# A sixth pair of rows by seven quarter products in the first MLP product, and later sums of its activations

## The chip, the cores and the metric

One core of a Trainium2 chip runs one layer of a streaming encoder in float32, in one launch. The metric is the device time of that launch in microseconds.

## The reference

The layer has token mixers, a cross-attention and a gated MLP. The change lies in the MLP, on 512 tokens of 1024 channels, with 2816 gate and 2816 value channels:

```python
hf = _rms_norm(x, norm_ffn_pre[l])
u = _dwconv_causal(hf @ w_up[l], ffn_dw[l]) + ffn_dw_b[l]      # width 3
u_g, u_v = jnp.split(u, 2, axis=-1)
yff = (jax.nn.silu(u_g) * u_v) @ w_down[l]
x = x + _rms_norm(yff, norm_ffn_post[l])
```

## The kernel before

Every operand of a matrix product is split in a high part (a cast, `wh`, `hth`) and a remainder (`wl`, `htl`), and a product is three matmuls: high x high, high x remainder, remainder x high. ScalarE (ACT) makes the cast (L191 for weights), VectorE (DVE) the remainder (L192).

**The first product, `up_jobs`.** It runs over 22 rows `j`. A row has two blocks of 128 channels, gate and value; a plain block (`plain_jobs`) is 8 slices of the 1024 inputs by three matmuls over 512 tokens, in one PSUM bank taken from `mm` and `av` in turn. `done` then applies the width-3 convolution (an activation on ACT, two taps on DVE, L597), and at the value block `gated` multiplies silu(gate) by value into `ns.quart[j // 2]` (tiles `qa0` to `qa10`, one for two rows).

**Pairs, `seven_jobs`.** At a row in `SEVEN_AT` the blocks of gate and value are seen as a 2 x 2 matrix (gate and value by two halves of the inputs) times a 2 x 2 matrix (halves of inputs by halves of tokens). Seven quarter products, each 4 slices by three matmuls over 256 tokens, take the place of eight: `A11`, `A12`, `S2`, `S3`, `S1`, `S4`, `A22`. The weights' sums `su`, `wv`, `s` (L1692 to L1695) are formed on DVE from the raw weights `wg` and `wv`; the tokens' sums are formed once, in `token_terms`, and split in `split_terms` into tiles `t4` to `t7`, `res0` to `res2` and `qa10`. Products are added up in three banks (`sc` twice, `tr`) and taken out to `u` by copies on ACT and adds on DVE (L1685). The jobs of such a row are mixed with the two plain blocks of the row after it, so a pair covers rows `j` and `j + 1`. The first pair's raw weights are loaded by `load_pair` two rows ahead, those of the next in `second_weights`.

**Sums of `w_down`, class `Sums`.** The last product is also done by seven products in place of eight. Its weight sums are formed during the first product, in 33 steps (`load`, `add` on DVE L545 to L548, `store` to DRAM L552, on POOL's queue), each placed by a call of `step()` after a job's products. Raw weights, `su`, and the rows of `w_down` (`wp`, later `dw`) share one ring of seven tiles (`ring`).

**Activation sums, `quart_sums`.** For two rows `q` the last product needs x1 + x3, x0 - x1 and (x1 + x3) - x0 of the four quarters of `ns.quart[q]` (L1598 to L1600, DVE, 256 wide). They go to `term_tile`s. Before the change they start two rows after the last pair.

**The last product, `down_jobs`.** Phase 0 forms M1, M6, M5 and M7 over 11 steps `q` with two jobs each; phase 1 forms M2, M3 and M4, and `ends` adds them up, multiplies by the gain `ns.post`, adds the residual `ns.out` (loaded again by `reload`) and stores. `weights` and `activations` make the splits (L1808, L1809), `load` issues the loads on SP (L564) three jobs ahead.

**Order.** `run_blocks` calls each job's weights three jobs ahead of its products. The text of the program gives the priority; a planner, which computes due times of its own, decides the order of the instructions on each engine and each queue. `tc.issue_after` keeps an instruction behind a named one. An engine takes its instructions in the planned order, and so does SP with its loads.

Of the kernel before, what the change touches and what calls it, by code (L numbers as in the profile page):

```python
# [25 lines left out]
P = 128  # L26
# [10 lines left out]
WB = 2 * 520  # L37
LINE = 256
HALF_SHIFT = 16
SEVEN_AT = (5, 8, 11, 14, 17)  # L40
BIG = -float(2.0 ** 100)
LAMBDA_INIT = 0.8 - 0.6 * math.exp(-0.3 * 0)

# [41 lines left out]
def hybrid_layer(ctx: ExitStack, tc: tile.TileContext, a: dict, out: bass.AP):  # L85
    nc = tc.nc
    V, A, G, PE, SP = nc.vector, nc.scalar, nc.gpsimd, nc.tensor, nc.sync
# [10 lines left out]
    def bank(tag=None):  # L98
        if tag is None:
            turn_of.n += 1  # L100
            tag = "av" if turn_of.shared and turn_of.n % 2 else "mm"
        return psum.tile([P, 512], F32, tag=tag, name=f"ps_{tag}", bufs=2)
# [143 lines left out]
    def channel_major(ps, w, act, sl=slice(0, S)):  # L246

        hi, lo = w
        nk = hi.shape[1]
        for k in range(nk):  # L250
            mm3(ps[:, sl], hi[:, k, :], lo[:, k, :], act[0][:, k, sl], act[1][:, k, sl], k == 0, k == nk - 1)
            if k == 3 < nk - 1:
                bg.tick()
# [324 lines left out]
    def seven_banks(phase):  # L578
        names = (("M2", "sc"), ("M3", "tr"), ("M4", "mm")) if phase else (("M1", "sc"), ("M6", "tr"), ("M5", "mm"),
                                                                         ("M7", "av"))  # L580
        return {name: [bank(tag) for _ in range(2)] for name, tag in names}
# [543 lines left out]
    ns = SimpleNamespace()  # L1125
# [425 lines left out]
    def open_ffn():  # L1551
        bg.drain("n1")
        token_terms()
        close(ns.work_)
        close(ns.xp_)
        close(ns.xm_)
        ns.fp_, ns.fp = new_pool("ffn", False)
        ns.work = ns.fp
        ns.quart = [quart(q) for q in range(NF // 2 - 1)]

    def term_tile(i, dtype=F32):
        if i < NT:
            return ns.res.tile([P, 4, S // 2], dtype, tag=f"res{i}", name=f"t{i}")
        return ns.fp.tile([P, 4, S // 2], dtype, tag=f"t{i}", name=f"t{i}")
# [13 lines left out]
    def split_terms():  # L1578
        for i, places in enumerate(((4, 5), (6, 7), (0, 1), (2, None))):
            hi, lo = (quart(10, F32R) if n is None else term_tile(n, F32R) for n in places)  # L1580
            split(ns.terms[i], hi, lo)
            ns.terms[i] = hi, lo

    def quart_sums(n, behind):

        if ns.quart_sums is None:
            ns.quart_terms = [term_tile(i) for i in range(6)]
            ns.post = ns.quart_terms.pop().rearrange("p a b -> p (a b)")
            ns.quart_sums = []
            G.dma_start(ns.post, a["norm_ffn_post"][0].partition_broadcast(P))  # L1590
        for q in range(len(ns.quart_sums), min(n, NF // 2)):
            x = ns.quart[q]
            if q < 10:
                two = ns.quart_terms[q // 2][:, q % 2 * 2:q % 2 * 2 + 2]
            else:
                two = ns.fp.tile([P, S], F32, tag="s4", name="two").rearrange("p (a b) -> p a b", a=2)
            with tc.issue_after(behind):
                V.tensor_tensor(two[:, 0], x[:, 1], x[:, 3], ALU.add)  # L1598
                V.tensor_tensor(two[:, 1], x[:, 0], x[:, 1], ALU.subtract)
            V.tensor_tensor(x[:, 1], two[:, 0], x[:, 0], ALU.subtract)  # L1600
            ns.quart_sums.append(two.rearrange("p a b -> p (a b)"))
# [4 lines left out]
    def up_jobs():  # L1606
        st, held = {}, []
        seven = SEVEN_AT
        raws = {}
# [13 lines left out]
        def done(j, i, ps):  # L1623
            if i == 0:
                st[j] = ns.fp.tile([P, 2, S], F32, tag="c", name="c", bufs=2)
            first_and_taps(st[j], j, i, ps)
            if i == 1:
                gated(st[j], j)
# [14 lines left out]
        def step(n=1):  # L1643
            for _ in range(n):
                f, q = next(steps, (None, None))
                if f == ns.sums.add:
                    with tc.issue_after(st["taps"]):
                        f(q)
                elif f is not None:
                    f(q)  # L1650
# [6 lines left out]
        def plain(j, i):  # L1657
            return cols(w_up, i * DFF + j * P)

        def load_pair(j):  # L1660
            if j in seven:
                raws[j] = [ring(name="wg"), ring(name="wv")]
                for i, raw in enumerate(raws[j]):
                    SP.dma_start(raw.rearrange("p (k c) -> p k c", k=NK), plain(j, i)[0])

        def seven_jobs(j):
# [10 lines left out]
            def product(ps, name, b, first=True):  # L1677
                hi, lo = w[name]
                for k in range(4):
                    for i, (w_p, x_p) in enumerate(((hi, b[0]), (hi, b[1]), (lo, b[0]))):  # L1680
                        matmul(ps[:, :S // 2], w_p[:, k], x_p[:, k], first and i == k == 0, i == 2 and k == 3,
                               not first)

            def add(dst, ps):
                V.tensor_tensor(dst, dst, ps[:, :S // 2], ALU.add)  # L1685
# [25 lines left out]
            def first(_):  # L1711
                u = kept["u"] = ns.fp.tile([P, 2, 2, S // 2], F32, tag="u", name="u", bufs=2)
                x.update(x=bank("sc"), v=bank("sc"), w=bank("tr"))
                product(x["x"], "A11", old(0, 0))
                A.copy(u[:, 0, 0], x["x"][:, :S // 2])
                step()
                product(x["w"], "A12", old(1, 0))
                add(u[:, 0, 0], x["w"])

# [41 lines left out]
        def plain_jobs(j):  # L1761
            for i in range(2):
                def body(hi, lo, i=i):
                    if j > 1:
                        ps = bank()
                        channel_major(ps, (hi, lo), ns.hf)
                        done(j, i, ps)
                        if (j, i) == (seven[0] - 2, 0):
                            load_pair(seven[0])
                        if (j, i) >= (seven[0] - 2, 1):  # L1770
                            step()
                        if j > seven[-1] + 1:
                            quart_sums(2 * (j - seven[-1] - 2) + i + 1, st["taps"])
                        return
                    if (j, i) == (0, 0):
                        bg.drain("n0")
                    ps = bank(("mm", "sc")[i])
                    (channel_major if i or j else by_pass)(ps, (hi, lo), ns.hf, slice(0, S // 2))
                    held.append((j, i, ps, (hi, lo)))
                    if (j, i) == (1, 1):  # L1780
                        open_ffn()
                        for m, n, ps, w in held:
                            (channel_major if m or n else by_pass)(ps, w, ns.hf, slice(S // 2, S))
                            done(m, n, ps)
                        split_terms()
                yield *plain(j, i), body, V, same, HALF_SHIFT if j < 2 else 0

        j = 0
# [6 lines left out]
    def down_jobs():  # L1795
# [11 lines left out]
        def split_to(hi, lo, x):  # L1807
            A.copy(hi, x)  # L1808
            parts["low"] = V.tensor_tensor(lo, x, hi.bitcast(F32), ALU.subtract).ins  # L1809

        def reload():
            ns.out = [term_tile(t).rearrange("p a b -> p (a b)") for t in range(NT)]
            for t in range(NT):
                SP.dma_start(ns.out[t], ns.kept[t * P:(t + 1) * P, :])
# [150 lines left out]
        def body(phase, q, job, ws):  # L1965
            if (q, job) == (0, 0):
                banks.update(seven_banks(phase))
            if (phase, q, job) == (1, 2, 0):
                reload()
            if phase == 0 and job == 0:  # L1970
                quart_sums(len(ns.quart_sums) + 1, parts["low"])
            if phase and q >= pairs - hold:
                held.append((q, job, ws))
                if (q, job) == (pairs - 1, 1):
                    ends()
                return
            for (name, a), w in zip(SEVEN[phase, job], ws):
                for t in range(2):
                    step(name, t, q, a, w, phase)
            if (phase, q) == (0, pairs - 1):  # L1980
                middle(job)
# [51 lines left out]
```

## Time and profile before

| what | value |
| --- | --- |
| median of 3 runs | 1048.98 us (1048.38 to 1055.58) |
| the profiled execution | 1049.11 us, of which span 1047.3 us |
| TensorE (PE) | 1038.0 us busy, 99% |
| weight load (PEld) | 891.0 us, 85% |
| VectorE (DVE) | 832.9 us, 80% |
| ScalarE (ACT) | 527.1 us, 50% |
| GpSimd (POOL) | 167.2 us, 16% |
| moved by DMA | 167.31 MB, mean 160 GB/s |

An engine that is busy for 99% of the span sets the time; the others matter where they make it wait. Shares over the span hide the stages, so the MLP, from about 700 us to the end, is read by stretches.

### The profile page before, as it was taken

What the parts mean: (1) busy time and instruction counts of PE and PEld (TensorE: products, weight loads), DVE (VectorE), ACT (ScalarE), POOL (GpSimd) and SP (SyncE); (2) the same over time, 40 slices, a digit from 0 to 9 for tenths busy, and PEclk for the clock granted to TensorE, in tenths of its full rate; (3) what the DMA queues carried; (4) which work ended last, traced back from release to release, by engine and by line L of the source; (5) the groups of instructions that cost most, each with busy time, mean ns of one, the idle gap of its engine ahead of it and who ended that gap; (6) DMA issues with size and microseconds to landing.
All of it is one profiled execution on the core that took longest, in us unless ns stands there. A gap on an engine that the chain in (4) does not pass through costs nothing.

```text
span 1047.3 us, 15070 instructions
## 1 busy us (share of the span) xinstructions
PE 1038.0 (99%) x5475; PEld 891.0 (85%) x5475; DVE 832.9 (80%) x1377; ACT 527.1 (50%) x888; POOL 167.2 (16%) x309
## 2 busy tenths in 40 slices
PE   9999999999999999999999999999999999999997
PEld 8888888888888988888888899999888888888886
DVE  6899997667667567767577798788787898799896
ACT  5322222277465365655444565666444454455672
POOL 4000000300231334343011031030011120000001
PEclk9999999999999999999999999999999999999999
DMA  8854334652443363332358733246478777827652
GB/s 269 289 172 104 103 101 139 181 123 81 120 122 95 88 173 93 99 97 65 121 161 231 269 124 122 100 143 196 123 245 246 255 240 235 269 83 266 189 176 81
DMA packets 166529, 167.31 MB, mean 160 GB/s; under 512 B 6656, under 2 KB 136301, under 8 KB 166198
## 3 DMA queue, kind: packets, MB, share of 16 engines
q1 hardware_dynamic: 154147, 124.10, 39.4%
q0 software_dynamic: 12160, 42.10, 12.3%
q8 instruction: 43, 0.70, 0.3%
q14 instruction: 33, 0.26, 0.1%
q10 hardware_dynamic: 146, 0.14, 0.0%
HBM read 141.13 MB, written 25.18 MB: 159 GB/s over the span
## 4 chain that ended last, share of the span: by engine, by line
PE 89%; DMA 4%; DVE 3%; issue 3%; ACT 0%; POOL 0%; SPq 0%; POOLq 0%; DVEq 0%; ACTq 0%
PE ps_mm L233 46%; PE ps_av L233 25%; PE ps_sc L233 10%; PE ps_tr L233 4%; PE ps_tr L237 2%; DMA sums<-wp 2%; DMA wr<-in_w_up 1%; DVE wl L192 1%; DVE c L597 1%; PE ps_mm L445 1%; PE ps_av L445 1%; PE ps_mm L387 0%; PE ps_sc L392 0%; ACT wh L191 0%; POOL wp L541 0%
## 5 line engine op out<-in xcount | busy, mean ns | idle before, releaser
L191 ACT CAST wh<-wr 128x1024 fp32r<-128x1024 f32 (+1 forms) x132 | 138.3, 1050 | 241.3 <-PE ps_mm L233 130.3
L192 DVE TENSOR_TENSOR wl<-wr,wh 128x1024 fp32r<-128x1024 f32 (+1 forms) x132 | 163.6, 1240 | 60.6 <-ACT wh L191 60.2
L233 PE MATMUL ps_mm<-hth,wh 128*128 128x512 f32 (+1 forms) x552 | 205.7, 380 | 0.2 <-ACT hth L156 0.2
L233 PE MATMUL ps_mm<-htl,wh 128*128 128x512 f32 (+1 forms) x552 | 205.3, 379 | 0.0
L233 PE MATMUL ps_mm<-hth,wl 128*128 128x512 f32 (+1 forms) x552 | 205.1, 379 | 0.0
L233 PEld LDWEIGHTS ps_mm<-hth,wl 128*128 128x128 f32 x552 | 102.0, 188 | 18.8
L233 PEld LDWEIGHTS ps_mm<-hth,wh 128*128 128x128 f32 x552 | 102.1, 188 | 18.2 <-ACT hth L156 0.8
L233 PEld LDWEIGHTS ps_mm<-htl,wh 128*128 128x128 f32 x552 | 102.1, 188 | 17.5
L233 PE MATMUL ps_av<-hth,wh 128*128 128x512 f32 (+1 forms) x312 | 116.3, 373 | 0.0
L233 PE MATMUL ps_av<-htl,wh 128*128 128x512 f32 (+1 forms) x312 | 116.2, 373 | 0.0
L233 PE MATMUL ps_av<-hth,wl 128*128 128x512 f32 (+1 forms) x312 | 116.1, 372 | 0.0
L668 DVE SCALAR_TENSOR_TENSOR y<-y,par,y 128x482 f32<-128x482 f32 (+29 forms) x120 | 83.2, 734 | 0.1
L233 PEld LDWEIGHTS ps_av<-hth,wl 128*128 128x128 f32 x312 | 58.6, 188 | 10.2
L233 PEld LDWEIGHTS ps_av<-htl,wh 128*128 128x128 f32 x312 | 58.6, 188 | 10.2
L233 PEld LDWEIGHTS ps_av<-hth,wh 128*128 128x128 f32 x312 | 58.6, 188 | 10.1
L1809 DVE TENSOR_TENSOR wl<-dw,wh 128x1024 fp32r<-128x1024 f32 x32 | 39.0, 1220 | 3.0 <-ACT wh L1808 2.2
L1061 POOL TENSOR_SCALAR fbias<-ck,cq 128x128 f32<-128x128 f32 (+3 forms) x32 | 28.2, 889 | 62.8 <-DVE st L1068 56.4
L1808 ACT CAST wh<-dw 128x1024 fp32r<-128x1024 f32 x32 | 33.4, 1049 | 9.2 <-PE ps_tr L233 6.6
L156 ACT CAST pth<-ps_tr 128x512 fp32r<-128x512 f32 (+3 forms) x56 | 23.5, 448 | 24.6 <-PE ps_tr L237 24.5
L269 POOL TENSOR_TENSOR st_m<-pm,nhalf 128x1 f32<-128x1 f32 x12 | 3.4, 287 | 180.3 <-ACT junk L1874 111.3
L157 DVE TENSOR_TENSOR ptl<-ps_tr,pth 128x512 fp32r<-128x512 f32 (+3 forms) x56 | 27.5, 512 | 5.7 <-ACT pth L156 5.3
L1619 ACT ACTIVATE c<-c 128x512 f32<-128x512 f32 x22 | 13.9, 631 | 35.7 <-DVE c L597 35.7
(553 smaller groups left out, 2418.5 us busy)
## 6 DMA issues: line engine op xcount, KB each, us to landing
wr<-in_w_in SPq DMA_DIRECT2D x38, 512.0 KB
wr<-in_w_up SPq DMA_DIRECT2D x34, 512.0 KB
wr<-in_w_gate SPq DMA_DIRECT2D x32, 512.0 KB
wp<-in_w_down POOLq DMA_DIRECT2D x22, 512.0 KB, 6.3
sums<-wp POOLq DMA_DIRECT2D x22, 512.0 KB, 5.0
dw<-sums SPq DMA_DIRECT2D x44, 256.0 KB
wr<-in_w_branch SPq DMA_DIRECT2D x16, 512.0 KB
wide<-in_w_out SPq DMA_DIRECT2D x12, 512.0 KB
```

What stands on the lines that cost most here:

```text
L156: A.copy(hi, ps)
L157: V.tensor_tensor(lo, ps, hi.bitcast(F32), ALU.subtract)
L191: order(A.copy(hi, raw[:, :n]))
L192: low.tensor_tensor(lo, raw[:, :n], hi.bitcast(F32), ALU.subtract)
L233: PE.matmul(ps, lhs, rhs, start=start, stop=stop, skip_group_check=more)
L237: PE.transpose(ps, x, ident[:n, :n])
L445: keep(PE.matmul(banks[c][:, :S // 2], w[p == 1][:, k, c * P:(c + 1) * P], ht[p == 2][:, i * 4 + k, :S // 2], start=(i, p, k) == (0, 0, 0) ...
L668: ins = V.scalar_tensor_tensor(dst[:, s:], src[:, :S - s], pc("conv_dw", k * 4 + j), dst[:, s:], ALU.mult, ALU.add)
L1061: G.tensor_scalar(bias[:, :w], ck[j][:, :w], -1.0, cq[:, qt, head:head + 1], ALU.mult, ALU.add)
L1619: A.activation(c[:, 0], c[:, 0], AF.Silu)
L1808: A.copy(hi, x)
L1809: parts["low"] = V.tensor_tensor(lo, x, hi.bitcast(F32), ALU.subtract).ins
```

## The change

A sixth pair is done by seven quarter products, and the pairs begin one row earlier. In `first` of a pair one `step()` goes. `quart_sums` takes tiles one by one (3, 6, 7, 0, 1), is called for two row pairs in the row ahead of the last pair and for two more in the row behind it, and leaves the rest to the last product. The load of the gain `norm_ffn_post` goes from the first call of `quart_sums` to step 5 of phase 0, into tile 5.

```diff
-SEVEN_AT = (5, 8, 11, 14, 17)
+SEVEN_AT = (4, 7, 10, 13, 16, 19)
...
         if ns.quart_sums is None:
-            ns.quart_terms = [term_tile(i) for i in range(6)]
-            ns.post = ns.quart_terms.pop().rearrange("p a b -> p (a b)")
-            ns.quart_sums = []
-            G.dma_start(ns.post, a["norm_ffn_post"][0].partition_broadcast(P))
+            ns.quart_terms, ns.quart_sums = [], []
         for q in range(len(ns.quart_sums), min(n, NF // 2)):
             x = ns.quart[q]
             if q < 10:
+                if q % 2 == 0:
+                    ns.quart_terms.append(term_tile((3, 6, 7, 0, 1)[q // 2]))
                 two = ns.quart_terms[q // 2][:, q % 2 * 2:q % 2 * 2 + 2]
...
                 product(x["x"], "A11", old(0, 0))
                 A.copy(u[:, 0, 0], x["x"][:, :S // 2])
-                step()
                 product(x["w"], "A12", old(1, 0))
...
                             step()
-                        if j > seven[-1] + 1:
-                            quart_sums(2 * (j - seven[-1] - 2) + i + 1, st["taps"])
+                        if j == seven[-1] - 1:
+                            quart_sums(i + 1, st["taps"])
+                        if j > seven[-1]:
+                            quart_sums(i + 3, st["taps"])
...
+        def load_post():
+            ns.post = term_tile(5).rearrange("p a b -> p (a b)")
+            G.dma_start(ns.post, a["norm_ffn_post"][0].partition_broadcast(P))
...
                 banks.update(seven_banks(phase))
+            if (phase, q, job) == (0, 5, 0):
+                load_post()
             if (phase, q, job) == (1, 2, 0):
                 reload()
```

## Prediction

> **What bounds the kernel now.** I read the page first, then a table of stretches cut at the stages of the MLP, then the order of time on the tensor engine, and last the waits of PE, SP and DVE around the pairs that the change touches.
>
> ```profile
> span 1047.3 us, 15070 instructions
> PE 1038.0 (99%) x5475; PEld 891.0 (85%) x5475; DVE 832.9 (80%) x1377; ACT 527.1 (50%) x888; POOL 167.2 (16%) x309
> L191 ACT CAST wh<-wr 128x1024 fp32r<-128x1024 f32 (+1 forms) x132 | 138.3, 1050 | 241.3 <-PE ps_mm L233 130.3
> ```
>
> TensorE is busy for 1038.0 of 1047.3 us. The question is thus only how much matrix work goes away and whether PE starts to wait anywhere for what replaces it. By stretches (one pair of the first product with the plain row behind it, the fifth pair, the plain rows 19 to 21, phase 0 of the last product):
>
> ```profile
> core 0: us, PE busy (x) PEld busy (x) DVE busy (x) ACT busy (x) POOL busy (x), PEclk, DMA share, GB/s
> 753.70:785.40 31.70, 31.70 (x181) 27.90 (x180) 26.55 (x37) 14.60 (x20) 4.27 (x8) 1.00 0.66 217
> ...
> 848.80:880.50 31.70, 31.70 (x182) 27.83 (x181) 27.35 (x39) 15.00 (x21) 4.81 (x9) 1.00 0.85 278
> 880.50:902.20 21.70, 21.40 (x131) 18.74 (x130) 16.94 (x24) 8.03 (x13) 2.67 (x5) 1.00 0.78 252
> 902.20:934.90 32.70, 32.70 (x150) 27.18 (x149) 28.61 (x45) 15.81 (x22) 0.00 (x0) 1.00 0.45 135
> 934.90:994.90 60.00, 60.00 (x266) 49.53 (x265) 53.39 (x80) 39.87 (x57) 0.00 (x0) 1.00 0.67 214
> ```
>
> PE is busy through each of them but for 0.3 us in the fifth pair. DVE is the next engine: 26.55 us of 31.70 in the first pair's stretch, 27.35 in the fourth, 28.61 of 32.70 in the three rows at the end, 53.39 of 60.00 in phase 0 of the last product. ACT stays at half in the first product and two thirds in phase 0. The DMA share climbs to 0.85 while the sums of w_down are loaded and stored beside the weights, and is 0.45 in the last three rows. The one wait of PE that the view of waits shows in this whole part, and the chain that leads to it:
>
> ```profile
> PE ps_sc L233 <- DVE u L1685: 0.3, 1, 0.3
> ```
>
> ```profile
> 886.12 3.56 DMA sums<-wp
> 889.68 0.02 SPq L564
> ...
> 891.00 6.95 DMA wr<-in_w_up
> ...
> 898.03 1.06 ACT wh L191
> ...
> 899.12 1.23 DVE wl L192
> ...
> 901.00 0.34 DVE u L1685
> ...
> 901.38 1.65 PE ps_sc L233 x12
> ```
>
> The reader is to see here a store of sums (886.12) that a load on SP (L564) waits for, because the load takes the ring slot which the store empties; behind that, in the same queue, a weight load of the first product (891.00, 6.95 us), then its cast on ACT, its remainder on DVE (899.12), DVE's add into u behind that (901.00), and PE 0.3 us late. So before the change the lead of the weights in the fifth pair is already used up, and the price was 0.3 us.
>
> **The change part by part.**
>
> *One more pair, minus two plain rows.* Rows 4/5, 7/8, 10/11, 13/14, 16/17 and 19/20 become pairs, where 5/6, 8/9, 11/12, 14/15 and 17/18 were. A plain row is two blocks of 24 matmuls over 512 tokens; the first row of a pair is 7 products of 12 matmuls over 256 tokens.
>
> ```profile
> 748.39 5.44 PE ps_av L233 x24
> 753.83 1.41 PE ps_sc L233 x12
> ```
>
> By these rows a block is 5.44 us, so a row is 10.88; a quarter product is 1.41, so seven are 9.87, and the pair saves 10.88 - 9.87 = 1.01 us. A second way takes the pairs themselves, by the first matmul of product A11 in the first, the second and the fifth:
>
> ```profile
> 753.66 0.28 PE L233 MATMUL ps_sc<-hth,wh 128*128 128x256 f32 x1
> ...
> 785.42 0.28 PE L233 MATMUL ps_sc<-hth,wh 128*128 128x256 f32 x1
> ...
> 880.50 0.28 PE L233 MATMUL ps_sc<-hth,wh 128*128 128x256 f32 x1
> ```
>
> From the first to the fifth are 126.84 us for four periods, 31.71 each; less a plain row of 10.88, a pair takes 20.83 us in place of 21.76. That is 0.93 us saved, and it holds whatever small waits a pair brings with it. I take -0.93; the bounds are -0.88 (the first period alone, 31.76) and -1.01.
>
> A rule of the Trainium skill speaks against cutting matmuls shorter: "TensorE: Matmul & The Clock Gate", section "Wait — 56ns, not 53.3ns?", says that a warm matmul takes its columns at 2.4 GHz plus about 2.5 ns, however many columns there are. By its figures, as an estimate, 48 x 215.8 ns less 84 x 109.2 ns would leave a gain of 1.19 us. The trace has such a fixed cost and a larger one (1.41 / 12 = 117.5 ns and 5.44 / 24 = 226.7 ns, so 8.3 ns for each matmul cut in two), so the rows decide.
>
> *What the added pair asks of DVE and ACT.* Beside a plain row, the first row of a pair has one more remainder over 1024 (three in place of two), one over 512 (s4l), four sums of weights over 512 and three adds of 256 into u; its four taps and its product remain.
>
> ```profile
> L192 DVE TENSOR_TENSOR wl<-su,wh 128x1024 fp32r<-128x1024 f32 x5 | 6.1, 1220 | 0.9 <-ACT wh L191 0.9
> L1685 DVE TENSOR_TENSOR u<-u,ps_sc 128x256 f32<-128x256 f32 x10 | 4.1, 414 | 0.0
> L1693 DVE TENSOR_TENSOR su<-su,wg 128x512 f32<-128x512 f32 x5 | 3.5, 690 | 0.1
> L157 DVE TENSOR_TENSOR s4l<-s,s4h 128x512 fp32r<-128x512 f32 x5 | 3.4, 683 | 0.0
> L1599 DVE TENSOR_TENSOR t<-qa 128x256 f32<-128x256 f32 x5 | 2.1, 420 | 0.0
> L1598 DVE TENSOR_TENSOR t<-qa 128x256 f32<-128x256 f32 x5 | 2.1, 415 | 0.0
> L1600 DVE TENSOR_TENSOR qa<-t,qa 128x256 f32<-128x256 f32 x4 | 1.7, 421 | 0.0
> ```
>
> That is 1.22 + 0.68 + 4 x 0.69 + 3 x 0.41 = 5.9 us of DVE, an upper value, since each instruction's record reaches a little into the next. Of the activation sums (L1598 to L1600, 0.42 + 0.42 + 0.42 = 1.26 us for a row pair) six were placed in the rows after the last pair and four are now, so 2.5 us go from this product to the last. The cover in rows 19 to 21 is 32.70 - 28.61 = 4.1 us of idle DVE; the need is 5.9 - 2.5 = 3.4 us. It fits by 0.7 us, which is thin. In phase 0 of the last product 53.39 + 2.5 = 55.9 us of 60.0 stand. It fits too, because the sums no longer have to come early: each phase 0 step of the last product asks for one, and the four ahead are four steps of lead. Cost taken: 0. If the cover in the rows is gone, the late thing would be the taps of row 21, which still read the PSUM bank that M7 or M5 needs, and the price is the whole shortage of up to 5.9 - 4.1 = 1.8 us. ACT gets one more cast of 1.05 us, a half one and four short copies, with 17 us idle in 32.7: 0.
>
> *The sums of w_down.* A step less in `first` makes four steps for a pair in place of five; the first step comes a row earlier (row 2). Counting the 33 steps through the rows, the last store was issued in the fifth pair's second job (row 17/18) and will be issued in row 18, ahead of the sixth pair. Between pairs there are six steps per three rows in place of seven, so the crowded stretches (DMA share 0.85) lose a seventh of the sums' traffic and of DVE's work on them. What moves the other way is the end: the last two stores now fall just ahead of the last pair, whose two raw weights and their sum also sit in the same seven-slot ring (`dw`), and the first loads of the last product must wait for these slots.
>
> ```profile
> SPq L564 <- DMA sums<-wp: 8.1, 4, 3.7
> ```
>
> Four such waits are there now, 8.1 us in all on SP, with nothing on PE beyond the stall shown. The weights queued behind L564 on SP are those of the plain rows; two tiles (`wr`) of lead cover them. Bounds: -0.3 us (the present stall disappears because the traffic is thinner) to +3.7 us (one longest wait, uncovered, next to the last pair). I take 0, nearest to the rows, since waits of 8.1 us have cost only that stall.
>
> *Where sums and gain lie.* The sums go to tiles 3, 6, 7, 0 and 1 in place of 0 to 4. Tile 3 is empty after the splits; 6, 7, 0 and 1 hold terms of products S2 and S3, done before row 21. The row pair 10 takes the tile of A22's low term while A22 is still to come in the sixth pair, so the product of row 20 waits for A22; that is one quarter product (1.41 us) right behind row 20's last matmuls, shorter than row 20's own taps on DVE, behind which its product stands anyway. If it did wait, u's add, the taps of row 19 and the remainder of row 21's weights would queue behind it on DVE, for at most 1.41 us. I take 0. The reload of the residual waits longer for tiles 0 and 1, but it is used only in the tail. 0.
>
> *The output gain* goes from the end of the sums to step 5 of phase 0.
>
> ```profile
> t<-in_norm_ffn_post POOLq DMA_DIRECT2D x1, 512.0 KB, 9.2
> ```
>
> Its 9.2 us are needed after step 10, five steps of 5.4 us later. 0. POOL has nothing queued behind it there: its next work in the page is in the second phase.
>
> *The sum.* The profiled execution took 1049.11 us with a span of 1047.3, so 1.8 us lie around it; its own time is 0.13 above the median of 1048.98. 1049.11 - 0.93 = 1048.2 us for the changed kernel, against the median a difference of -0.8.
>
> **The rivals.**
>
> 1. *The stall goes too.* Sums thinner by a seventh leave the weight loads of the pairs on time; the pair's -0.93 and the 0.3 us of the chain both go: 1047.9; with what a pair takes beyond its matmuls gone in all six (6 x 0.08), 1047.4. For it: the present stall follows a store of sums. Against: the crowding moves to row 18 instead of vanishing.
>
> 2. *DVE becomes the bound at the end.* The sixth pair stands one row before the last product, where DVE has 4.1 us left, and the start of phase 0 needs its remainders at once. With the whole of 5.9 us due there, 1.8 us come back: 1048.2 + 1.8 = 1050.0, slower than before. It decides if the sums of activations are planned ahead of the remainders. For it: DVE at 53.39 of 60.00 in phase 0. Against: the four sums of lead.
>
> 3. *SP is blocked by the late stores* (slower). The last two stores of sums are a row later; L564 loads stand on SP ahead of the weight loads for rows 19 to 21. If one longest wait of 3.7 us meets a moment without lead, as one did in the fifth pair, PE stands for what is not covered: 1048.2 + 3.7 = 1051.9 at most, 1050.1 with half of it covered. It decides once the wait is longer than the two `wr` tiles' lead. Against: the DMA share of 0.45 in the last rows, which is room to catch up.
>
> 4. *Nothing is saved.* A new wait inside each of the six pairs, shifted by one row against the splits of the terms in rows 2 and 3, of 0.15 us each would eat the gain: 1049.1. For it: the first pair now starts only two rows after the terms are formed.
>
> **How the numbers follow.** Forecast 0.45, rival 1 0.12, rival 2 0.15, rival 3 0.20, rival 4 0.08. The likeliest time is 1048.2, its own range 1047.7 to 1048.9 (the runs of before but the highest differ by 0.6). The range to be given takes rival 1 with half a microsecond of that spread below (1046.9) and rival 3 nearly whole above (1051.6). A measurement of this kernel can tell about 1% (10 us) from no change. No case reaches 1% faster: the whole of the pair's work is 0.93 us; 0.01. For 1% slower three longest waits on SP would have to come uncovered, or a schedule that I do not see; 0.05. Within 1%: 0.94.
>
> **What would show it.** Right: 84 more matmuls over 256 tokens and 48 fewer over 512; six A11 starts some 31.7 us apart, the first near 742.8; the last product's first matmul near 934.0 in place of 934.9; PE's last near 1037.7. DVE in the last pair and row 21 above 90% of the stretch. Wrong: a wait of PE over 1 us between row 18 and step 4 of phase 0, on DVE (rival 2) or behind a late `wr` load (rival 3); pairs at more than 20.9 us (rival 4); or a gap in the first pair, should the split terms not be ready.

## The result, and the profile after

| | before | after |
| --- | --- | --- |
| median of 20 runs each | 1049.34 us (1047.95 to 1055.58) | 1047.20 us (1046.30 to 1047.97) |
| ratio after / before | | 0.9976, 95% interval 0.9968 to 0.9985 |
| span of the profiled execution | 1047.3 us | 1046.2 us |

The change is faster by 0.15 to 0.32%, some 2.1 us between the medians, where 0.9 us had been worked out. It lies within 1%, and the direction was right, the size was not. The spread of the runs, 7.6 us before, is 1.7 us after.

The page of the kernel after, its busy times and its chain that ended last:

```profile
span 1046.2 us, 15153 instructions
PE 1036.5 (99%) x5511; PEld 891.6 (85%) x5511; DVE 836.9 (80%) x1386; ACT 530.6 (51%) x894; POOL 181.6 (17%) x309
...
PE 98%; DMA 1%; DVE 0%; issue 0%; ACT 0%; POOLq 0%; DVEq 0%; POOL 0%; SPq 0%; ACTq 0%
```

The chain of before, from its page:

```profile
PE 89%; DMA 4%; DVE 3%; issue 3%; ACT 0%; POOL 0%; SPq 0%; POOLq 0%; DVEq 0%; ACTq 0%
```

TensorE's busy time falls by 1.5 us and DVE's rises by 4.0 us. PE does 36 matmuls more, as 84 over 256 tokens for 48 over 512 ask. The share of PE in the chain rises from 89% to 98%, so by this chain little but PE's own work decides any more. The stretches of the first product and of phase 0 (columns as in the table of before):

```profile
743.70:775.50 31.80, 31.80 (x181) 27.94 (x181) 27.30 (x39) 14.96 (x22) 4.26 (x8) 1.00 0.76 244
...
870.40:902.00 31.60, 31.60 (x181) 27.77 (x180) 26.52 (x38) 15.13 (x21) 3.19 (x6) 1.00 0.71 225
902.00:922.90 20.90, 20.90 (x125) 18.52 (x125) 17.19 (x27) 10.28 (x15) 1.59 (x3) 1.00 0.67 216
922.90:933.80 10.90, 10.90 (x60) 9.40 (x59) 9.81 (x16) 5.86 (x9) 0.00 (x0) 1.00 0.60 180
933.80:993.80 60.00, 60.00 (x266) 49.53 (x265) 55.05 (x85) 40.17 (x57) 0.00 (x0) 1.00 0.65 203
```

No stretch has idle time on PE. The DMA share lies between 0.71 and 0.76 from the first pair to the fifth, where it climbed to 0.85 before. DVE has 17.19 + 9.81 us of 31.8 in the last pair and row 21.

The first matmul of the first, the second and the sixth pair, and that of the last product, in the timeline of PE after:

```profile
743.74 0.28 PE L233 MATMUL ps_sc<-hth,wh 128*128 128x256 f32 x1
...
775.52 0.28 PE L233 MATMUL ps_sc<-hth,wh 128*128 128x256 f32 x1
...
902.05 0.28 PE L233 MATMUL ps_sc<-hth,wh 128*128 128x256 f32 x1
...
933.73 0.39 PE L233 MATMUL ps_sc<-wh,wr 128*128 128x512 f32 x1
```

And that of the last product before:

```profile
934.85 0.39 PE L233 MATMUL ps_sc<-wh,wr 128*128 128x512 f32 x1
```

From the first pair to the last product are 933.73 - 743.74 = 189.99 us. Before, the same rows 4 to 21 were 934.85 - 753.66 = 181.19 us and one plain row of 10.88, together 192.07. **The first product is thus shorter by 2.08 us**, while the spans differ by 1.1 only. The rest is hidden by what stands ahead of the pairs: this execution reached the MLP 0.96 us later (743.74 against 753.66 - 10.88 = 742.78), and the view of waits of PE has a wait far ahead of the change that the execution of before did not have:

```profile
PE ps_tr L237 <- DVE par L501: 0.8, 1, 0.8
```

The stretch is a far steadier measure than the span: in two more profiled executions of the kernel after it was 189.99 and 189.99 us again. From here on "stretch" is that time, from the first pair's first matmul to the last product's first.

### The profile page after: what moved, and what is told of

The parts are those of the page before. It is cut to its first block, busy times and chain, and to the rows that moved or that the text cites. A ratio compares the mean times of both kernels' runs of the same rounds, so it can differ in the third digit from the quotient of the medians.

```text
span 1046.2 us, 15153 instructions
## 1 busy us (share of the span) xinstructions
PE 1036.5 (99%) x5511; PEld 891.6 (85%) x5511; DVE 836.9 (80%) x1386; ACT 530.6 (51%) x894; POOL 181.6 (17%) x309
## 4 chain that ended last, share of the span: by engine, by line
PE 98%; DMA 1%; DVE 0%; issue 0%; ACT 0%; POOLq 0%; DVEq 0%; POOL 0%; SPq 0%; ACTq 0%
PE ps_mm L233 48%; PE ps_av L233 28%; PE ps_sc L233 13%; PE ps_tr L233 5%; PE ps_tr L237 2%; DMA wide<-in_w_out 1%; PE ps_mm L445 1%; PE ps_mm L387 0%; PE ps_sc L392 0%; PE ps_av L445 0%; ACT hth L156 0%; DVE o L1923 0%; PE ps_tr L429 0%; DVE wide L546 0%; POOLq L2035 0%
## 5 line engine op out<-in xcount | busy, mean ns | idle before, releaser
L192 DVE TENSOR_TENSOR wl<-wr,wh 128x1024 fp32r<-128x1024 f32 (+1 forms) x130 | 161.1, 1241 | 65.5 <-ACT wh L191 65.3
L233 PE MATMUL ps_mm<-hth,wh 128*128 128x512 f32 (+1 forms) x544 | 202.6, 380 | 0.2 <-ACT hth L156 0.2
L233 PE MATMUL ps_mm<-htl,wh 128*128 128x512 f32 (+1 forms) x544 | 202.4, 379 | 0.0
L233 PE MATMUL ps_mm<-hth,wl 128*128 128x512 f32 (+1 forms) x544 | 202.1, 379 | 0.0
L233 PE MATMUL ps_av<-hth,wh 128*128 128x512 f32 (+1 forms) x304 | 113.2, 373 | 0.0
L233 PE MATMUL ps_av<-htl,wh 128*128 128x512 f32 (+1 forms) x304 | 113.2, 372 | 0.0
L233 PE MATMUL ps_av<-hth,wl 128*128 128x512 f32 (+1 forms) x304 | 113.1, 372 | 0.0
L269 POOL TENSOR_TENSOR st_m<-pm,nhalf 128x1 f32<-128x1 f32 x12 | 13.5, 1128 | 159.5 <-ACT junk L1878 90.4
L1061 POOL TENSOR_SCALAR fbias<-ck,cq 128x128 f32<-128x128 f32 (+3 forms) x32 | 28.2, 890 | 63.0 <-DVE st L1068 56.6
L233 PE MATMUL ps_sc<-t,wh 128*128 128x256 f32 x168 | 32.8, 278 | 0.0
```

The source lines that it names most:

```text
L192: low.tensor_tensor(lo, raw[:, :n], hi.bitcast(F32), ALU.subtract)
L233: PE.matmul(ps, lhs, rhs, start=start, stop=stop, skip_group_check=more)
L269: G.tensor_tensor(m, parts[0], eps[:, :n], ALU.add)
L1061: G.tensor_scalar(bias[:, :w], ck[j][:, :w], -1.0, cq[:, qt, head:head + 1], ALU.mult, ALU.add)
```

## The experiments

All stretches at once, from the same two matmuls in the timeline of PE of each kernel; rows are shown where a verdict rests on them. A stretch from row 5 has one plain row, 10.88 us, less than one from row 4.

| kernel | first row | first pair's first matmul | last product's first | stretch |
| --- | --- | --- | --- | --- |
| before | 5 | 753.66 | 934.85 | 181.19 |
| e1, a step fewer in each pair | 5 | 755.51 | 935.62 | 180.11 |
| e4, other parts of the change alone | 5 | 753.36 | 934.75 | 181.39 |
| e9, su in its own tile | 5 | 753.38 | 934.88 | 181.50 |
| e13, additions on POOL | 5 | 753.68 | 936.26 | 182.58 |
| e14, the first job's step moved | 5 | 753.88 | 934.15 | 180.27 |
| e15, the fourth job's step moved | 5 | 752.77 | 935.76 | 182.99 |
| after | 4 | 743.74 | 933.73 | 189.99 |
| after, second and third chip | 4 | 743.39, 743.16 | 933.38, 933.15 | 189.99, 189.99 |
| e2, the step put back | 4 | 742.20 | 933.87 | 191.67 |
| e3, five pairs | 4 | 742.35 | 933.35 | 191.00 |
| e5, seven pairs | 4 | 743.19 | 932.68 | 189.49 |
| e7, stores twice | 4 | 743.82 | 934.00 | 190.18 |
| e8, more on DVE | 4 | 743.28 | 933.86 | 190.58 |
| e10, a ring of six | 4 | 742.93 | 933.27 | 190.34 |
| e11, seven pairs, earlier | 4 | 743.03 | 932.56 | 189.53 |
| e12, stores twice and more on DVE | 4 | 742.61 | 933.50 | 190.89 |

Within a stretch, the time from one pair's first matmul to the next pair's can be read in the same timeline. Wherever no matmul starts late, it is 31.76, 31.68 or 31.63 us in every kernel with a plain row between its pairs (31.78 in the first pair of a kernel that begins at row 4, which has a break as below without gaining by it). Which of them it is goes with the order in which the planner has put the matmuls, and not with a wait. A piece of 24 quarter-product matmuls without a break, here in e8, starts one every 118 ns:

```profile
812.39 0.52 PE L233 MATMUL ps_sc<-t,wh 128*128 128x256 f32 x3
...
815.22 0.40 PE L233 MATMUL ps_mm<-hth,wh 128*128 128x512 f32 x1
```

In after, three matmuls over 512 tokens stand behind the first two of the 24, and the other 22 start one every 113 ns:

```profile
813.66 0.39 PE L233 MATMUL ps_sc<-t,wh 128*128 128x256 f32 x2
...
816.15 0.40 PE L233 MATMUL ps_mm<-hth,wh 128*128 128x512 f32 x1
```

Periods of 31.76 us have no such break, those of 31.68 us one and those of 31.63 us two. Why the matmuls go faster behind a break was not asked. So a difference of 0.05 or 0.13 us for a pair is one of order, fixed before the kernel runs, and a real wait shows as a matmul that starts late.

Theory A was that the sixth pair is worth its 0.9 to 1.0 us and that one step of the sums fewer per pair thins the traffic that made weights late; theory B that the later activation sums, or the sixth pair alone, carry the gain.

**The steps without the pair.** The kernel before with

```diff
                 A.copy(u[:, 0, 0], x["x"][:, :S // 2])
-                step()
                 product(x["w"], "A12", old(1, 0))
```

> The kernel before with one step of the sums of w_down fewer in each of its five pairs (four in place of five), nothing else. Theory A (the extra 1.2 us came from the sums' traffic being spread thinner, which ends the late weight load in the fifth pair): the pair from its A11 start (880.50 before) takes about 20.9 us in place of 21.7, and the time falls by 0.8 to 1.5 us against before, without any sixth pair. Theory B (the crowding only moves to the row where the last sums are then stored, and the gain is from the later activation sums or from the sixth pair): within 0.3 us of before, with a wait of PE somewhere in rows 17 to 20.

Median 1048.17 us against 1049.92 of before on the same chip, ratio 0.9981 (0.9972 to 0.9990). PE's first pair and last product:

```profile
755.51 0.28 PE L233 MATMUL ps_sc<-hth,wh 128*128 128x256 f32 x1
...
935.62 0.40 PE L233 MATMUL ps_sc<-wh,wr 128*128 128x512 f32 x1
```

The stretch is 180.11 us, 1.08 less than before: 0.90 from the fifth pair's first matmul on, where no matmul starts late any more, and 0.18 in the second and the fourth pair, by the order alone. One deleted call brings half of the change's gain.

**The change without its sixth pair**, `SEVEN_AT = (4, 7, 10, 13, 16)` in the kernel after:

> The kernel after with the sixth pair (rows 19 and 20) taken out: five pairs from row 4, four steps each, late activation sums, late load of the gain. Theory A: only the pair's 0.93 us go back, so 0.9 us slower than after and about 1.2 us faster than before; every pair near 20.8 us. Theory B: as slow as before if the sixth pair was the whole gain, that is some 2 us slower than after.

Median 1047.96 us, ratio to before 0.9978 (0.9967 to 0.9989).

```profile
742.35 0.28 PE L233 MATMUL ps_sc<-hth,wh 128*128 128x256 f32 x1
...
933.35 0.39 PE L233 MATMUL ps_sc<-wh,wr 128*128 128x512 f32 x1
```

The stretch is 191.00 us, or 180.12 without row 4: as in the experiment above to 0.01 us, so the pairs' shift by a row, the later activation sums and the later load of the gain add nothing here. Against the kernel after the sixth pair is worth 191.00 - 189.99 = 1.01 us, and 1.08 + 1.01 is the 2.08 of the whole change to 0.01.

**The rest of the change alone**: the kernel after with the pairs at 5, 8, 11, 14, 17 and the `step()` in `first` put back.

> The kernel after with the five pairs of before at their old rows and five steps in each: what is left of the change are the activation sums in other tiles (two row pairs ahead of the last pair, two behind it, the rest in the last product) and the later load of the gain. Theory A: no gain, within 0.3 us of before, the fifth pair near 21.7 us and PE waiting once in it. Theory B, that this part carries the extra gain: 1 to 1.5 us faster than before.

Median 1050.18 us, ratio 1.0000 (0.9988 to 1.0012).

The stretch is 181.39 us, 0.2 more than before, and again two matmuls start late in the fifth pair. The activation sums and the gain's load carry no gain; theory B is out.

**The step put back** into `first` of the kernel after, with its six pairs:

> The kernel after with the step of the sums put back into the first job of each pair: six pairs, five steps each. Theory A: the six pairs keep their 0.9 us, but weight loads come late again while the sums run (up to the fifth pair), so 0.7 to 1.5 us slower than after, about 0.9 faster than before. Theory B: as after, within 0.3 us.

Median 1049.49 us, ratio to before 0.9986 (0.9977 to 0.9995).

The stretch is 191.67 us, 1.68 more than after. The wait, at 813.27 us, is now in the third pair and not in the fifth, so it is not bound to the end of the sums:

```profile
PE ps_sc L233 <- ACT u L1714: 0.8, 1, 0.8
```

**What the step harms.** The next runs ask for the cause. The kernel after once more on the same chip as three others:

> The kernel after, unchanged, on the chip of the three runs beside it, so that they can be compared with it. Theory A: 2.0 to 2.8 us below before, every pair with its plain row 31.6 to 31.8 us, no wait of PE in the first product of the MLP, and a narrow spread of runs.

189.99 us, median 1047.30 against 1050.40 of before there, ratio 0.9963 (0.9951 to 0.9975). On the chip of three more:

> The kernel after, unchanged, on the chip of the three runs beside it: some 1047.2 us, no wait of PE between 715 us and the last product.

189.99 us, median 1046.95 against 1049.66, ratio 0.9972 (0.9962 to 0.9982).

*More bytes*: in the kernel after every store of the sums is done twice.

```diff
                 self.queue.dma_start(self.dram[q * P:(q + 1) * P, i * D:(i + 1) * D], x)
+                self.queue.dma_start(self.twice[q * P:(q + 1) * P, i * D:(i + 1) * D], x)
```

> The kernel after with every store of the sums of w_down done twice (a second copy to a place of its own in DRAM that nobody reads): 11.5 MB more on the DMA queues, no work more on PE, DVE or ACT. If the late loads of before came from crowded DMA queues, waits of PE come back in the pairs: 0.5 to 3 us slower than after, with a wide spread of runs. If they came from DVE's work on the sums, nothing: within 0.3 us of after.

Median 1047.55 us, 0.25 above after on that chip, and the highest run 1049.73. The fourth and the fifth pair, nearly, in a table of stretches:

```profile
838.00:870.00 32.00, 32.00 (x183) 28.07 (x183) 28.46 (x41) 15.51 (x22) 6.35 (x12) 1.00 0.93 317
870.00:902.00 32.00, 32.00 (x183) 28.12 (x182) 26.27 (x38) 14.95 (x21) 5.29 (x10) 1.00 0.92 299
```

The DMA share is 0.93 and 0.92, far above the 0.85 of before, and the stretch grows by 0.19 us only, to 190.18. No matmul starts late; four of the pairs take 31.68 us in place of 31.63, which is the order again. Theory A, that crowding by bytes makes the wait, falls.

*More work on DVE*: in the kernel after, two more instructions in each `add`.

```diff
             V.tensor_tensor(b21, b21, b11, ALU.subtract)
+            for t in (b12, b21):
+                V.tensor_tensor(t, t, t, ALU.max)
```

> The kernel after with two DVE instructions over 512 more in every step that adds the sums (the maximum of a tile with itself, values unchanged): 1.4 us of DVE more for each of 11 row pairs, no bytes more. That is at least what the fifth step per pair had asked of DVE. If DVE's work on the sums was what made before wait, waits of PE come back, 0.5 to 2 us slower than after. If it was the DMA queues: within 0.4 us of after.

Median 1048.06 us, 0.76 above after.

The stretch is 190.58 us, 0.59 more, and again no matmul starts late: every pair behind the first takes 31.76 us, the order without a break. DVE's work does not bring the wait back; what the 0.59 us come from is the order that the planner chose beside it. *Both burdens at once*:

> The kernel after with both burdens at once: every store of the sums done twice, and two DVE instructions over 512 more in each step that adds sums. Each alone left PE without a wait. Theory D (PE waits when the weight loads land late and DVE has no room to catch up, both together): waits of PE come back in the pairs, 0.5 to 3 us slower than after, with a wider spread of runs. If neither matters and only the planner's order of five steps does: within 1 us of after, no wait of PE.

Median 1048.79 us on another chip, ratio to before there 0.9983 (0.9971 to 0.9995).

The stretch is 190.89 us, 0.90 more than after. Of these, 0.59 are the order of e8. The rest is in the sixth pair, where one matmul starts late, at 910.05 us, behind a weight load of PE that waits for a remainder from DVE:

```profile
PEld ps_sc L233 <- DVE wl L192: 0.5, 1, 0.5
```

Theory D had named waits in the pairs; one small one came, of 0.3 us in the stretch, in one pair of six. More bytes and a busy DVE together can thus make a weight late, but not by the 0.9 us of before.

*A wait for a ring slot.* In the views of waits of ACT and DVE of the kernel before, between 740 and 934 us, stand

```profile
ACT wh L191 <- DMA wr<-in_w_up: 27.7, 10, 5.1
...
DVE su L1692 <- DMA sums<-wp: 6.4, 3, 3.1
```

and of these the second is missing after, which made theory C: `su` waits for a slot, and DVE behind it in order. The kernel before with `su` in a tile of its own:

```diff
-su, s4 = kept["su"], kept["s4"] = ring(name="su"), ...
+su, s4 = kept["su"], kept["s4"] = term_tile(3).rearrange("p a b -> p (a b)"), ...
```

> The kernel before with one thing changed: the sum of a pair's weights (su) goes to term tile 3, which is free while the pairs run, in place of a slot of the ring of seven. Theory C (in before DVE stands in order behind su, which waits until a store of sums of w_down has emptied a ring slot; in the trace 6.4 us in three waits, against none in after): these waits of DVE are gone, the fifth pair takes 20.8 to 21.0 us, 1 to 2 us faster than before with five steps per pair and no sixth pair. Theory A (the traffic itself crowds the queues): within 0.5 us of before, weight loads still late.

Median 1049.84 us, ratio 1.0000 (0.9989 to 1.0010).

```profile
753.38 0.28 PE L233 MATMUL ps_sc<-hth,wh 128*128 128x256 f32 x1
...
934.88 0.39 PE L233 MATMUL ps_sc<-wh,wr 128*128 128x512 f32 x1
```

```profile
ACT wh L191 <- DMA wr<-in_w_up: 28.2, 10, 5.2
```

DVE's wait is gone and the stretch is 181.50 us, nothing gained. Theory C falls; ACT's wait for weights of the first product (28.2 us, ten times) stays. From the other side, the kernel after with `bufs=6` for the ring:

> The kernel after with the ring cut from seven slots to six, nothing else. Theory C: with the raw weights (2), su (1) and two row pairs of sums (4) one slot is missing now even at four steps per pair; su or the raw weights wait for stores of sums, DVE stands behind them, PE waits: 0.5 to 4 us slower than after. Theory A (bytes decide): the same bytes move, within 0.5 us of after.

Median 1048.24 us, 1.29 above after.

The stretch is 190.34 us. The 0.35 us more are the order again (31.68 and 31.76 in turn), with no matmul late, so the slot is not what made before slow. The median rises by more than that, which the trace does not explain.

*DVE made free*: the kernel before with the sums' `add` on GpSimd (`G` in place of `V`).

> The kernel before with the four sums of each step of w_down done by GpSimd (POOL) in place of DVE; five pairs, five steps, the same bytes. Theory D: DVE has 2.7 us more room for each row pair, so the late loads are caught up and the fifth pair takes 20.8 to 21.0 us: 0.8 to 2 us faster than before, with loads landing as late as in before. If the late loads alone decide: within 0.5 us of before. If POOL's instructions are far slower and hold back its own loads and stores behind them: slower by 1 us or more, with the sums ready late.

Median 1050.99 us, ratio 1.0008 (0.9994 to 1.0022).

The stretch is 182.58 us, 1.39 more than before, with two late matmuls in the fifth pair. That POOL's own loads and stores, which stand behind its additions, come later for it is likely and was not taken apart; the run says nothing for a freer DVE.

*The place of the step.* The kernel before with the step of `first` moved to the plain row between the pairs, so that three rows still have seven steps:

```diff
-                step()                       # in first, after A11
...
                         if (j, i) >= (seven[0] - 2, 1):
-                            step()
+                            step(1 + i * (j > seven[0]))
```

> The kernel before with the step of a pair's first job moved to the value block of the plain row between the pairs: four steps in a pair and three in a plain row, so seven in three rows as in before, and as many steps done at the end of every row. If the rate of seven steps in three rows (two and a third row pairs of sums) crowds the loads: as before, within 0.5 us, the loads of w_down landing after 6 us or more. If the place of the step in the pair's first job was the harm: 1 to 2 us faster than before, like the kernel with that step taken out.

Median 1048.61 us, ratio to before 0.9981 (0.9968 to 0.9993).

```profile
753.88 0.28 PE L233 MATMUL ps_sc<-hth,wh 128*128 128x256 f32 x1
...
934.15 0.39 PE L233 MATMUL ps_sc<-wh,wr 128*128 128x512 f32 x1
```

```profile
ACT wh L191 <- DMA wr<-in_w_up: 15.2, 8, 4.5
...
DVE su L1692 <- DMA sums<-wp: 5.8, 3, 2.7
```

The stretch is 180.27 us, 0.92 less than before, at the rate of before, and no matmul starts late. DVE's wait for the slot is here as long as in before (5.8 us), once more no harm; ACT's wait for weights is 15.2 us against 27.7. And its counterpart, where the step of `third` moves to the plain row and that of `first` stays:

> The kernel before with the step of a pair's fourth job (after S1) moved to the value block of the plain row between the pairs, while the step of its first job stays. If it is the first job's place that harms (its step falls 1.4 us after the pair's start, another one 4.2 us and a third 5.6 us after it): as before, within 0.5 us, the stretch from the first pair to the last product near 181.2 us. If five steps in a pair are one too many wherever they are: 180.1 to 180.3 us in that stretch, 1 to 2 us faster than before.

Median 1051.60 us against 1049.47, ratio 1.0019 (1.0007 to 1.0032).

```profile
752.77 0.28 PE L233 MATMUL ps_sc<-hth,wh 128*128 128x256 f32 x1
...
935.76 0.39 PE L233 MATMUL ps_sc<-wh,wr 128*128 128x512 f32 x1
```

The stretch is 182.99 us, 1.80 more than before, with late matmuls in the fourth and the fifth pair. Neither of the two outcomes given had a loss; with the step of `first` in place, moving another one out of the pair made it worse. Still, the two kernels have the same number of steps in a pair, the same rate, and 2.7 us between them: **the step in `first` does the harm by its place**. All six kernels that keep it (before, e2, e4, e9, e13, e15) lose 0.9 us or more to late matmuls in the third, fourth or fifth pair; of the others, e11 and e12 alone have any, of 0.3 us. The weights show it too. ACT's wait for weights of the first product, in the row given above, is 27.0 to 29.3 us in these six but for e13 (12.2), and 5.0 to 20.9 us in every kernel without the step.

How the place makes weights late is less clear. One reading comes from the order on POOL's queue. Stores of sums in the kernel before, in the one with the step of `third` moved, and after, all ahead of the last pair of before or in the pairs after:

```profile
860.36 2.34 POOL L552 DMA_DIRECT2D sums<-wp  x4 [6.14 <-DVE wp L547]
```

```profile
862.23 0.54 POOL L552 DMA_DIRECT2D sums<-wp  x1 [5.16 <-DVE wp L547]
863.43 1.13 POOL L552 DMA_DIRECT2D sums<-wp  x2 [0.67 <-DVE wp L548]
864.76 0.53 POOL L552 DMA_DIRECT2D sums<-wp  x1 [0.19 <-issue]
```

```profile
849.54 1.08 POOL L552 DMA_DIRECT2D sums<-wp  x2 [7.65 <-issue]
...
859.10 0.53 POOL L552 DMA_DIRECT2D sums<-wp  x1 [5.84 <-DVE wp L547]
862.10 0.53 POOL L552 DMA_DIRECT2D sums<-wp  x1 [2.46 <-DVE wp L548]
```

In the first two, four stores of 512 KB are issued within 2.3 and 3.1 us, and a weight load of the first product goes out right into them. In the second kernel the chain that leads to the late matmuls of the fifth pair has it:

```profile
865.63 8.80 DMA wr<-in_w_up
```

8.80 us for 512 KB. After, two stores start together at most, and the pattern is the same in every pair. But such bunches stand without a late matmul, too. The first line is from the first pair of before, the second from the fifth pair of the kernel with the step of `first` moved, the others from the doubled stores, where four start together in every pair:

```profile
762.88 2.34 POOL L552 DMA_DIRECT2D sums<-wp  x4 [6.11 <-DVE wp L547]
```

```profile
891.57 2.34 POOL L552 DMA_DIRECT2D sums<-wp  x4 [11.82 <-DVE wp L547]
```

```profile
848.02 0.54 POOL L553 DMA_DIRECT2D sums<-wp  x1 [4.78 <-DVE wp L548]
848.55 0.54 POOL L555 DMA_DIRECT2D sums_twice<-wp  x1
849.07 0.53 POOL L553 DMA_DIRECT2D sums<-wp  x1
849.59 0.53 POOL L555 DMA_DIRECT2D sums_twice<-wp  x1
```

So four stores at once are not enough. And other late matmuls hang on other waits: by the chain in the prediction the last one of before on a load that stood behind SP's wait for a store, and that of the kernel with the step put back on `su`, which waits for a store. That the step's place harms is shown; by which transfers it does so stays open. The Trainium skill, "DMA: Bandwidth & Descriptors", section "Issuing engines are not separate DMA queues", says that transfers started by different engines share the same 16 DMA engines and interleave; the trace fits this, with the 8.80 us of a load on SP's queue beside stores on POOL's.

**A seventh pair.** The kernel after with pairs at 4, 6, 9, 12, 14, 17, 19 (activation sums from row 16):

> The kernel after with a seventh pair (rows 4, 6, 9, 12, 14, 17, 19, so that some pairs follow each other without a plain row between), four steps each; the first call for the activation sums is at row 16. Theory A (a pair is worth its 0.9 to 1.0 us of matrix work as long as the weights stay ahead): 0.9 us faster than after. Rival (DVE is the bound where pairs touch: 16.5 us for a pair and 3.6 us for its share of the sums, in 20.8 us): PE waits at the touching pairs, 0 to 2 us slower than after.

Median 1048.88 us, 1.58 above after on that chip.

```profile
PE ps_mm L233 <- ACT wh L1808: 1.2, 1, 1.2
```

The stretch falls by 0.50 us, half a pair's worth, to 189.49. No matmul in it starts late; the quarter products start one every 117.3 ns in the mean against 116.4 after, which makes some 0.5 us over seven pairs, so the missing half is mostly order. PE then waits 1.2 us for a cast at the start of phase 0. With the pairs at 4, 6, 8, 11, 13, 16, 18, farther from the last product:

> The kernel after with seven pairs again, but at rows 4, 6, 8, 11, 13, 16 and 18, so that the plain rows 20 and 21 stand between the last pair and the last product (the first activation sums at row 15). If the loss with the seventh pair came from DVE being behind where the last product begins, this is 0.5 to 1.0 us faster than after; if it came from the touching pairs themselves, PE waits at rows 6 to 9 and it is 0 to 2 us slower than after.

Median 1047.77 us against 1046.95 of after, ratio to before 0.9976 (0.9966 to 0.9986).

The stretch is 189.53 us, 0.46 less than after, with late starts of 0.3 us in all near 863 us and no wait in phase 0; yet the median is 0.8 above that of after. The intervals of the two overlap, and what takes the 0.46 us back in the other executions stays open. No version that was run beats the kernel after.

## Why the prediction was right and wrong, point by point

- **The pair** (taken -0.93, bounds -0.88 to -1.01) was worth 1.01 us, the far bound. The prediction put the 0.08 us between down to small waits in a pair. They are no waits: the periods of before are 31.76, 31.76, 31.63 and 31.68 us by the order of the matmuls alone, and after has the order of 31.63, (902.05 - 775.52) / 4, in four of its six pairs. That the bound was met to 0.01 us is in part luck, since it counts every quarter product at 117.5 ns a matmul, where some run at 113.
- **The step that failed is the sum of the w_down edit, taken at 0.** Its gain is 1.08 us, in the first rival's direction, which had 0.12 and whose farther price, 1047.4 us, came nearest. Two errors stand in it. The mechanism was given as traffic thinner by a seventh; the run with moved steps has the same rate and nearly the whole gain, and the run with doubled stores has far more traffic without a late matmul. It is the place of one call, and by which transfers it works stays open. And the term was mis-sized: the wait was priced by the view of waits, 0.3 us, where the fifth pair's length was in a quoted row, 21.70 us from 880.50 to 902.20 against the 20.83 worked out for a pair, so 0.87. In the timeline of PE before, three matmuls of that pair start late, at 886.43, 899.40 and 901.38 us; with the ones behind them they stand 0.23, 0.16 and 0.57 us farther apart than usual. The view of waits names the last of the three only, and it counts 0.30 of its 0.57 us, because the record of the matmul ahead reaches into the gap. What remains of the 1.08 us is mostly order.
- **The last pair's DVE work** was taken at no cost, and no matmul was late for it: DVE was 27.0 of 31.8 us busy, 85%, where above 90% was expected. Phase 0 came to 55.05 us of DVE, against 55.9 worked out, with PE busy through all of it.
- **SP's loads behind the late stores** (rival 3, 0.20) stood there again: SP's loads (L564) wait 7.1 us for them, 4.7 at longest, where it was 8.1 and 3.7 before, and no matmul is late. The last two stores were expected in row 18, ahead of the sixth pair. They came inside that pair, which begins at 902.05 us:

```profile
910.71 0.53 POOL L552 DMA_DIRECT2D sums<-wp  x1 [15.89 <-DVE wp L547]
912.25 0.53 POOL L552 DMA_DIRECT2D sums<-wp  x1 [1.01 <-DVE wp L548]
```

- **The load of the gain** made no matmul late. It was not at step 5 of phase 0 at all; the planner drew it forward to where tile 5 came free:

```profile
916.01 0.53 POOL L1813 DMA_DIRECT2D t<-in_norm_ffn_post  x1 [3.23 <-PE ps_sc L233]
```

- **The start of the last product** was expected near 934.0 and came at 933.73, in an execution that ran 0.96 us late, so by its own terms at 932.8.
- **The medians** differ by 2.1 to 3.1 us on three chips, at or above the 2.08 us of the traces. Before is known by one trace and by runs from 1047.3 to 1055.6; after, the runs of each chip lie within 1.7 us. That the waits of before vary between executions would fit both; only one execution of before was traced, so this is not shown.

## What to carry to other kernels

Measure a bottleneck engine's loss as the length of a repeated piece against its undisturbed length, not by the waits that a view lists; here the row of the fifth pair had 0.87 us where the list of waits had 0.3. Before a small difference is called a wait, compare the order of the instructions: here another order of the same matmuls made up to 0.13 us for a pair. When background work is dealt out in steps among jobs, where a step stands can matter more than how many there are: try the same rate with the steps elsewhere. A pattern that stands beside a slow spot, as four stores at once do here, is to be looked for in the fast runs as well before it is called the cause. And take the parts of a change out one by one before explaining it: one deleted line was half of this one.

## What was not expected

The stretch repeats between executions and chips to 0.01 us (189.99 three times) when no matmul is late, so differences of 0.2 us in it can be read, while the runs' medians of the same kernel lie 0.35 us apart. And a DMA share of 0.92 to 0.93 (317 GB/s) was borne without a late matmul in e7, where before had three with 0.85 at most.
